# Rotary embedding on one core: rows in pairs, the last tile stored whole, 63 no-ops at the top of two programs

## The chip, the cores and the metric

The kernel runs on one core of a Trainium2 chip. The metric is the device time of one execution in microseconds (us); the time before is the median of 13 runs. The core has five engines that run their own instruction streams and meet at semaphores: PE (matrix multiply), DVE (VectorE), ACT (ScalarE), POOL (GpSimd) and SP, which here only issues DMAs. Sixteen DMA engines, called rings below, move data between the HBM and the on-chip memory SBUF. PSUM is a smaller on-chip memory that PE writes its results to[...].

## What is computed

```
def setup_inputs():
    batch, seq, dim = (16, 512, 1024)
    num_heads = 16
...
x = x.reshape(batch, seq, num_heads, head_dim)
x1, x2 = (x[..., :half_dim].copy(), x[..., half_dim:].copy())
...
rotated = np.concatenate([x1 * cos - x2 * sin, x1 * sin + x2 * cos], axis=-1)
```

Everything is fp32. `x` and the output are 33.6 MB each; `cos` and `sin` are 512 x 32 tables, one row for each position of the sequence. Each element of the output is one product with cos and one product with sin (of the element in the other half of its head), added.

## The kernel before

**Tiles.** Two batches make a tile of 128 partitions: 64 partitions for each batch, and on each partition 8 rows of 1024 elements that lie one behind the other in HBM (32 KB). There are 8 tiles, numbered t = 0 to 7, in a pool of 5 buffers (`BUFS`), and a tile is changed in place: loaded, rotated, stored from the same buffer. One DMA of a whole tile moves 4 MB, a piece of 32 KB for each partition.

**The SP queue.** All loads and stores are issued by SP, in program order: rows 0 to 2 of tile 0, the sin and cos tables, the rest of tile 0, tiles 1 to 4 (L75, L84, L85), and then the stores (L79). After the store of tile 2 come the loads of tiles 5, 6 and 7, each of which waits until the store that frees its buffer (tile 0, 1, 2) has landed. An instruction of SP that waits holds up all that is behind it. The last tile is stored in two halves, `LAST_OUT = (4, 8)`: rows 0 to 3 as soon as they are done, then rows 4 to 7.

**The tables.** One identity matrix doubled (L106) and two matmuls (L107, L108) spread the 64-partition tables over 128 partitions in the PSUM tile `tab`. DVE makes `sns` from it in SBUF (L110, L111), sin with a minus sign for the first half of a head, and one row of that back in `tab` (L115).

**The rows of a tile** go one by one, k = 0 to 7, in one of three ways:

- Rows 1, 2, 3, 5, 6 and 7: POOL multiplies the row, halves swapped, by sin into a buffer `b` (L168). DVE multiplies the row by cos into the PSUM tile `pd` (L186), and later adds the two into the row (`add`, L148). A list `pending` holds the addition back by a row or so.
- Row 4: the same product on POOL (L168); DVE makes the cos product in two halves of 512 into PSUM tiles `ps` (L174); PE adds `b` to each half by a matmul with the identity (L181), and ACT copies the half from PSUM into the row (L182).
- Row 0: as row 4, but DVE makes the sin product itself, in place (L179), and POOL does nothing.

So POOL has 7 products of 1024 elements for each tile, and DVE 17 instructions: 6 at L186, 6 at L148, 4 at L174, 1 at L179. There are 6 buffers `b`, 2 tiles `pd` (1024 elements) and 3 `ps` (512).

**Order between tiles.** `finish(t - 1)` is called after row 0 of tile t: it makes the addition that is still pending, and issues the store of tile t - 1. In the middle of the kernel (t = 3) ACT issues four small DMAs with 15, 14, 12 and 8 pieces of 64 bytes (L193); nothing reads what they load.

Of the kernel before, what the change touches and what calls it, by code (L numbers as in the profile page):

```python
# [8 lines left out]
FP32 = mybir.dt.float32  # L9
BF16 = mybir.dt.bfloat16  # L10
ALU = mybir.AluOpType

NB = 2
BUFS = 5
B_BUFS = 6
BANK = 512


PE_ROWS = ((0, 4), (0, 4))

DVE_B = ((0,), (0,))

FIRST = (3, 8)
LAST_OUT = (4, 8)

SMALL = (15, 14, 12, 8)


@with_exitstack
def kernel(  # L30
    ctx: ExitStack,
    tc: tile.TileContext,
    x: bass.AP,
    cos: bass.AP,
    sin: bass.AP,
    num_heads: bass.AP,
    out: bass.AP,
):

    nc = tc.nc
    P = nc.NUM_PARTITIONS
    batch, seq, dim = x.shape
    nh = num_heads
    hd = dim // nh
    half = hd // 2
    PB = P // NB  # L50
    KK = seq // PB
    NT = batch // NB
    F = KK * dim

    x_v = x.rearrange("(t b) (p k) d -> t (b p) (k d)", b=NB, k=KK)
    out_v = out.rearrange("(t b) (p k) h d -> t (b p) (k h d)", b=NB, k=KK)
    cos_v = cos.rearrange("(p k) j -> p (k j)", k=KK)
    sin_v = sin.rearrange("(p k) j -> p (k j)", k=KK)

    fixed = ctx.enter_context(tc.tile_pool(name="fixed", bufs=1))  # L60
    xp = ctx.enter_context(tc.tile_pool(name="xp", bufs=BUFS))
    bp = ctx.enter_context(tc.tile_pool(name="bp", bufs=B_BUFS))
    pfix = ctx.enter_context(tc.tile_pool(name="pfix", bufs=1, space=bass.MemoryType.PSUM))
    pe = ctx.enter_context(tc.tile_pool(name="pe", bufs=3, space=bass.MemoryType.PSUM))
    pd = ctx.enter_context(tc.tile_pool(name="pd", bufs=2, space=bass.MemoryType.PSUM))

    ctx.enter_context(tc.manual_schedule())

    tiles = [None] * NT

    def load(t, lo=0, hi=KK):
        if tiles[t] is None:
            tiles[t] = xp.tile([P, F], FP32, name="xt")
        s = slice(lo * dim, hi * dim)
        nc.sync.dma_start(out=tiles[t][:, s], in_=x_v[t][:, s])  # L75

    def store(t, lo=0, hi=KK):
        s = slice(lo * dim, hi * dim)
        nc.sync.dma_start(out=out_v[t][:, s], in_=tiles[t][:, s])  # L79

    load(0, 0, FIRST[0])
    sin_sb = bp.tile([P, dim], FP32, name="b")[:PB, : KK * half]
    cos_sb = bp.tile([P, dim], FP32, name="b")[:PB, : KK * half]
    nc.sync.dma_start(out=sin_sb, in_=sin_v)  # L84
    nc.sync.dma_start(out=cos_sb, in_=cos_v)  # L85
    for lo, hi in zip(FIRST, FIRST[1:]):
        load(0, lo, hi)
    for t in range(1, BUFS):
        load(t)

    ident = fixed.tile([P, P], FP32)
    make_identity(nc, ident)
    zero = fixed.tile([P, BANK], BF16)
    nc.vector.memset(zero, 0.0)  # L94
    for i in range(3):
        ps = pe.tile([P, BANK], FP32, name="ps")
        nc.tensor.matmul(out=ps, lhsT=zero[:, :P], rhs=zero, start=True, stop=True)  # L97

    spare = fixed.tile([16, len(SMALL), 16], FP32)
    sns = fixed.tile([P, KK, 2, half], FP32)  # L100
    tab = pfix.tile([P, BANK], FP32)
    cos_t = tab[:, : KK * half]
    sin_t = tab[:, KK * half : 2 * KK * half]
    spread = fixed.tile([PB, P], FP32)
    for b in range(NB):
        nc.vector.tensor_copy(out=spread[:, b * PB : (b + 1) * PB], in_=ident[:PB, :PB])  # L106
    nc.tensor.matmul(out=sin_t, lhsT=spread, rhs=sin_sb, start=True, stop=True)  # L107
    nc.tensor.matmul(out=cos_t, lhsT=spread, rhs=cos_sb, start=True, stop=True)  # L108
    sin_k = sin_t.rearrange("p (k j) -> p k j", k=KK)
    nc.vector.tensor_scalar_mul(out=sns[:, :, 0, :], in0=sin_k, scalar1=-1.0)  # L110
    nc.vector.tensor_copy(out=sns[:, :, 1, :], in_=sin_k)  # L111
    on_dve = sorted(set(DVE_B[0]) | set(DVE_B[1]))
    sns_t = tab[:, KK * half : KK * half + len(on_dve) * hd]
    for i, k in enumerate(on_dve):
        nc.vector.tensor_copy(out=sns_t[:, i * hd : (i + 1) * hd], in_=sns[:, k])  # L115

    def cos_b(k, n):
        c = cos_t[:, k * half : (k + 1) * half]
        return bass.AP(tensor=c.tensor, offset=c.offset, ap=[c.ap[0], [0, n], [1, half]])

    def over_heads(s):
        return bass.AP(tensor=s.tensor, offset=s.offset, ap=[s.ap[0], [0, nh], [1, hd]])

    def swapped(r, n):
        return bass.AP(
            tensor=r.tensor, offset=r.offset + half, ap=[r.ap[0], [hd, n], [-half, 2], [1, half]]
        )

    def swapped_signed(k):

        i = on_dve.index(k)
        s = sns_t[:, i * hd : (i + 1) * hd]
        return bass.AP(
            tensor=s.tensor, offset=s.offset + half, ap=[s.ap[0], [0, nh], [-half, 2], [1, half]]
        )

    def pairs(r):
        return r.rearrange("p (a j) -> p a j", j=half)

    def halves(r):  # L140
        return r.rearrange("p (h a j) -> p h a j", a=2, j=half)

    pending = []

    def add(most):
        while len(pending) > most:
            r, ps, b = pending.pop(0)
            nc.vector.tensor_tensor(out=r, in0=ps, in1=b, op=ALU.add)  # L148

    def finish(t):  # L150
        add(0)
        lo = 0
        for hi in LAST_OUT if t == NT - 1 else (KK,):
            store(t, lo, hi)
            lo = hi
        if t + 1 == NT - BUFS:
            for n in range(BUFS, NT):
                load(n)

    for t in range(NT):  # L160
        xt = tiles[t]
        for k in range(KK):
            r = xt[:, k * dim : (k + 1) * dim]
            own = k in DVE_B[t % 2]
            if not own:
                b = bp.tile([P, dim], FP32, name="b")
                sk = sns[:, k].rearrange("p a j -> p (a j)")
                nc.gpsimd.tensor_tensor(out=halves(b), in0=swapped(r, nh), in1=over_heads(sk), op=ALU.mult)  # L168
            if k in PE_ROWS[t % 2]:
                parts = []  # L170
                for c in range(0, dim, BANK):
                    ps = pe.tile([P, BANK], FP32, name="ps")
                    rc = r[:, c : c + BANK]
                    nc.vector.tensor_tensor(  # L174
                        out=pairs(ps), in0=pairs(rc), in1=cos_b(k, BANK // half), op=ALU.mult
                    )
                    parts.append((ps, rc, swapped(rc, BANK // hd) if own else b[:, c : c + BANK]))
                if own:
                    nc.vector.tensor_tensor(out=halves(r), in0=halves(r), in1=swapped_signed(k), op=ALU.mult)  # L179
                for ps, rc, rhs in parts:  # L180
                    nc.tensor.matmul(out=ps, lhsT=ident, rhs=rhs, start=False, stop=True, skip_group_check=True)  # L181
                    nc.scalar.copy(out=rc, in_=ps)  # L182
            else:
                add(1)
                ps = pd.tile([P, dim], FP32, name="pd")
                nc.vector.tensor_tensor(out=pairs(ps), in0=pairs(r), in1=cos_b(k, 2 * nh), op=ALU.mult)  # L186
                pending.append((r, ps, b))
            if k == 0 and t > 0:
                finish(t - 1)
            add(1)  # L190
        if t == NT // 2 - 1:
            for i, n in enumerate(SMALL):
                nc.scalar.dma_start(out=spare[:n, i], in_=sin_v[:n, :16])  # L193
    finish(NT - 1)


# [33 lines left out]
```

## Time and profile before

| | us |
|---|---|
| median of 13 runs | 162.5 (162.28 to 163.29) |
| the profiled execution | 162.66 |
| its span, first to last instruction | 160.9 |
| DVE busy | 141.4 (88% of the span) |
| POOL busy | 130.3 (81%) |
| PE busy | 62.1 (39%) |
| ACT busy | 20.0 (12%) |
| DMA packets, share of 16 rings | 97.8% of the span, 67.24 MB |

The span is shorter than the time of the same execution by 1.8 us, which lie before the first and behind the last instruction. An engine's busy time is the union of its instructions' times. The DMA share is the time of all packets over 16 rings times the span; a packet of a tile is one piece of one partition, 32 KB, or 16 KB where half a tile is stored.

### The profile page before, as it was taken

Reading aid. Unit: us, or ns where it says so; the run is one execution under the profiler, and the core shown is the slowest. Engines: PE = TensorE matmul, PEld = TensorE weight load, DVE = VectorE, ACT = ScalarE, POOL = GpSimd, SP = SyncE. Lnnn points to the kernel's source line nnn. Section 1 sums busy time; section 2 is a strip of 40 time slices with the busy share of each in tenths; the row PEclk is TensorE's granted clock in tenths of the full one; section 3 lists DMA queues with packets and bytes.
Section 4 is the critical chain, followed back from the end, with each engine's and each line's share of the span. In section 5 each row is a group of like instructions: output and inputs, shape, how many; then the busy total and the mean of one; then the engine's idle time right before and its main releaser. Section 6 shows DMA issues by size and latency. Waiting matters only on the chain. (4 is left out here: it accounts for less than half of the span.)

```text
span 160.9 us, 531 instructions
## 1 busy us (share of the span) xinstructions
PE 62.1 (39%) x71; PEld 19.9 (12%) x71; DVE 141.4 (88%) x142; ACT 20.0 (12%) x33; POOL 130.3 (81%) x62
## 2 busy tenths in 40 slices
PE   3136360536217350809044530817062712635000
PEld 0112010202011100202020200211020201120000
DVE  1059999999999999999999999999999999999700
ACT  0111120021102020111102020202011110202000
POOL 1039999999999999999999799999999799940000
PEclk9999955555856876595558555555555585557755
DMA  5999999999999899999999999999999999999993
GB/s 186 400 412 467 399 513 391 391 521 391 391 497 416 385 432 481 391 416 489 399 400 505 399 399 466 432 399 456 448 399 440 464 399 440 456 407 411 428 440 163
DMA packets 2852, 67.26 MB, mean 418 GB/s; under 512 B 418, under 2 KB 546, under 8 KB 546
## 3 DMA queue, kind: packets, MB, share of 16 engines
q1 hardware_dynamic: 2752, 67.24, 97.8%
q10 hardware_dynamic: 98, 0.00, 0.0%
q14 instruction: 2, 0.02, 0.0%
HBM read 33.69 MB, written 33.55 MB: 418 GB/s over the span
## 5 line engine op out<-in xcount | busy, mean ns | idle before, releaser
L168 POOL TENSOR_TENSOR b<-xt,sns 128x1024 f32<-128x1024 f32 x56 | 129.6, 2362 | 11.6 <-DVE sns L111 9.2
L186 DVE TENSOR_TENSOR pd<-xt,tab 128x1024 f32<-128x1024 f32 x48 | 58.1, 1225 | 0.8
L148 DVE TENSOR_TENSOR xt<-pd,b 128x1024 f32<-128x1024 f32 x48 | 58.4, 1217 | 0.0
L181 PE MATMUL ps<-xt,ident 128*128 128x512 f32 x32 | 29.6, 1079 | 49.1 <-issue 38.1
L181 PE MATMUL ps<-b,ident 128*128 128x512 f32 x32 | 29.0, 1061 | 29.7 <-DVE ps L174 27.1
L182 ACT COPY xt<-ps 128x512 f32<-128x512 f32 x32 | 18.8, 586 | 120.3 <-PE ps L181 120.3
L174 DVE TENSOR_TENSOR ps<-xt,tab 128x512 f32<-128x512 f32 x32 | 20.6, 688 | 0.0
L181 PEld LDWEIGHTS ps<-xt,ident 128*128 128x128 f32 x32 | 9.4, 324 | 68.7 <-issue 64.1
L181 PEld LDWEIGHTS ps<-b,ident 128*128 128x128 f32 x32 | 9.1, 312 | 49.4 <-issue 25.4
L179 DVE TENSOR_TENSOR xt<-xt,tab 128x1024 f32<-128x1024 f32 x8 | 9.8, 1222 | 0.4
L110 DVE TENSOR_SCALAR sns<-tab 128x256 f32<-128x256 f32 x1 | 0.4, 425 | 8.1 <-PE tab L108 8.1
L107 PE MATMUL tab<-b,spread 64*128 64x256 f32 x2 | 1.2, 696 | 5.0 <-DMA b<-in_sin_dram 5.0
L182 ACT ACT_TABLE_LOAD x1 | 1.3, 1283 | 7.4 <-DMA xt<-in_x_dram 7.4
L97 PE MATMUL ps<-zero 128*128 128x512 bf16 x3 | 1.5, 626 | 1.2 <-DVE zero L94 1.2
L107 PEld LDWEIGHTS tab<-b,spread 64*128 64x128 f32 x2 | 0.5, 306 | 5.8 <-issue 5.8
L108 PE MATMUL tab<-b,spread 64*128 64x256 f32 x2 | 1.1, 631 | 0.0
L94 DVE MEMSET zero<- 128x256 uint32 x1 | 0.3, 272 | 0.9 <-PEq L211 0.9
L108 PEld LDWEIGHTS tab<-b,spread 64*128 64x128 f32 x2 | 0.7, 333 | 0.2
L106 DVE COPY spread<-ident 64x64 f32<-64x64 f32 x2 | 0.3, 184 | 0.2 <-POOL ident masks.py:199 0.2
L97 PEld LDWEIGHTS <-zero 128*128 128x128 bf16 x3 | 0.3, 125 | 1.5 <-DVE zero L94 1.2
masks.py:197 POOL MEMSET ident<- 128x128 f32 x1 | 0.2, 204 | 0.3 <-POOLq L211 0.3
L111 DVE COPY sns<-tab 128x256 f32<-128x256 f32 x1 | 0.4, 415 | 0.0
(6 smaller groups left out, 0.9 us busy)
## 6 DMA issues: line engine op xcount, KB each, us to landing
xt<-in_x_dram SPq DMA_DIRECT2D x7, 4096.0 KB, 29.2
out_dram<-xt SPq DMA_DIRECT2D x7, 4096.0 KB, 28.0
out_dram<-xt SPq DMA_DIRECT2D x2, 2048.0 KB, 8.6
xt<-in_x_dram SPq DMA_DIRECT2D x1, 2560.0 KB
xt<-in_x_dram SPq DMA_DIRECT2D x1, 1536.0 KB, 6.6
b<-in_sin_dram SPq DMA_DIRECT2D x1, 64.0 KB, 6.3
b<-in_cos_dram SPq DMA_DIRECT2D x1, 64.0 KB, 5.9
spare<-in_sin_dram ACTq DMA_DIRECT2D x1, 0.9 KB, 7.2
```

The costliest lines, as they stand in the source:

```text
L97: nc.tensor.matmul(out=ps, lhsT=zero[:, :P], rhs=zero, start=True, stop=True)
L107: nc.tensor.matmul(out=sin_t, lhsT=spread, rhs=sin_sb, start=True, stop=True)
L108: nc.tensor.matmul(out=cos_t, lhsT=spread, rhs=cos_sb, start=True, stop=True)
L110: nc.vector.tensor_scalar_mul(out=sns[:, :, 0, :], in0=sin_k, scalar1=-1.0)
L111: nc.vector.tensor_copy(out=sns[:, :, 1, :], in_=sin_k)
L148: nc.vector.tensor_tensor(out=r, in0=ps, in1=b, op=ALU.add)
L168: nc.gpsimd.tensor_tensor(out=halves(b), in0=swapped(r, nh), in1=over_heads(sk), op=ALU.mult)
L174: nc.vector.tensor_tensor(out=pairs(ps), in0=pairs(rc), in1=cos_b(k, BANK // half), op=ALU.mult)
L179: nc.vector.tensor_tensor(out=halves(r), in0=halves(r), in1=swapped_signed(k), op=ALU.mult)
L181: nc.tensor.matmul(out=ps, lhsT=ident, rhs=rhs, start=False, stop=True, skip_group_check=True)
L182: nc.scalar.copy(out=rc, in_=ps)
L186: nc.vector.tensor_tensor(out=pairs(ps), in0=pairs(r), in1=cos_b(k, 2 * nh), op=ALU.mult)
```

## The change

- Rows 1 and 2, 4 and 5, 6 and 7 are handled two at a time: one POOL product, one DVE cos product and one DVE addition of 2048 elements for each pair. `pd` becomes one tile of 2048 elements.
- Row 3 takes the place of row 4 as the row that PE adds and ACT copies, in two halves that share one PSUM tile `pe_ps`.
- Row 0 has its cos product in one instruction of 1024 elements into `own_ps`, made in the tile before (for tile 0, ahead of the loop). PE adds it in two halves as before; ACT copies it in one instruction.
- The order inside a tile is written out. `pending` and `finish` are gone: the store of tile t is issued at the end of tile t.
- There are 3 buffers `b`, of 2048 elements. The tables' load takes one of them.
- The last tile is stored by one DMA.
- The four small DMAs of ACT are gone. Five DMAs with one piece of 64 bytes are issued by SP behind the load of tile 4; nothing reads what they load.
- The two copies at L106 become one.
- 63 no-op instructions stand at the top of DVE's program, and 63 at the top of POOL's.

```diff
-PE_ROWS = ((0, 4), (0, 4))
-DVE_B = ((0,), (0,))
+ROW_OWN, ROW_PE = 0, 3
+PAIRS = ((1, 2), (4, 5), (6, 7))
 FIRST = (3, 8)
-LAST_OUT = (4, 8)
-SMALL = (15, 14, 12, 8)
+LAST_OUT = (8,)
+EXTRA = 5
...
-    bp = ctx.enter_context(tc.tile_pool(name="bp", bufs=B_BUFS))
+    bp = ctx.enter_context(tc.tile_pool(name="bp", bufs=3))
...
-    pe = ctx.enter_context(tc.tile_pool(name="pe", bufs=3, space=bass.MemoryType.PSUM))
-    pd = ctx.enter_context(tc.tile_pool(name="pd", bufs=2, space=bass.MemoryType.PSUM))
+    pe = ctx.enter_context(tc.tile_pool(name="pe", bufs=1, space=bass.MemoryType.PSUM))
+    pd = ctx.enter_context(tc.tile_pool(name="pd", bufs=1, space=bass.MemoryType.PSUM))
...
     for t in range(1, BUFS):
         load(t)
+    spare = fixed.tile([1, EXTRA, 16], FP32)
+    for i in range(EXTRA):
+        nc.sync.dma_start(out=spare[:1, i], in_=sin_v[:1, :16])
+    for i in range(63):
+        nc.vector.nop(hint="pause")
+    for i in range(63):
+        nc.gpsimd.nop(hint="pause")
...
+    def sin_product(out, r, k, n):
+        s = sns[:, k : k + n].rearrange("p k a j -> p (k a j)")
+        if n == 1:
...
+        else:
+            sb = bass.AP(tensor=s.tensor, offset=s.offset, ap=[s.ap[0], [hd, n], [0, nh], [1, hd]])
+            o = out.rearrange("p (k h a j) -> p k h a j", k=n, a=2, j=half)
+            i = bass.AP(
+                tensor=r.tensor,
+                offset=r.offset + half,
+                ap=[r.ap[0], [dim, n], [hd, nh], [-half, 2], [1, half]],
+            )
+        nc.gpsimd.tensor_tensor(out=o, in0=i, in1=sb, op=ALU.mult)
+
+    def sin_rows(t, k, n):
+        b = bp.tile([P, 2 * dim], FP32, name="b")[:, : n * dim]
+        sin_product(b, rows(t, k, n), k, n)
+        return b
+
+    def pe_half(k, r, b):
+        cos_product(pe_ps, r, k)
+        pe_add(pe_ps, b)
+        nc.scalar.copy(out=r, in_=pe_ps)
+
+    def pair_product(t, k):
+        ps = pd.tile([P, 2 * dim], FP32, name="pd")
+        cos_product(ps, rows(t, k, 2), k, 2)
+        return ps, rows(t, k, 2)
+
+    def pair_sum(ps, r, b):
+        nc.vector.tensor_tensor(out=r, in0=ps, in1=b, op=ALU.add)
...
+    cos_product(own_ps, rows(0, ROW_OWN), ROW_OWN)
     for t in range(NT):
...
+        first, second, third = PAIRS
+        b1 = sin_rows(t, first[0], 2)
+        p1 = pair_product(t, first[0])
+        r0 = rows(t, ROW_OWN)
+        own_product(r0)
+        for ps, r in zip(parts(own_ps), parts(r0)):
+            pe_add(ps, swapped(r))
+        nc.scalar.copy(out=r0, in_=own_ps)
+        b3 = sin_rows(t, ROW_PE, 1)
+        b2 = sin_rows(t, second[0], 2)
+        pair_sum(*p1, b1)
+        h0, h1 = zip(parts(rows(t, ROW_PE)), parts(b3))
+        pe_half(ROW_PE, *h0)
+        p2 = pair_product(t, second[0])
+        b1 = sin_rows(t, third[0], 2)
+        pair_sum(*p2, b2)
+        pe_half(ROW_PE, *h1)
+        p1 = pair_product(t, third[0])
+        if t + 1 < NT:
+            cos_product(own_ps, rows(t + 1, ROW_OWN), ROW_OWN)
+        pair_sum(*p1, b1)
+        stores(t)
```

`cos_product`, `own_product` and `pair_sum` run on DVE, `sin_product` on POOL, `pe_add` is a matmul with the identity on PE. `stores(t)` issues the store of tile t and, behind that of tile 2, the loads of tiles 5 to 7, as `finish` did.

## The prediction, made before the result was known

> **What bounds the kernel now.** I read the page first: the rows of slices, the DMA queues, the costliest groups.
>
> ```profile
> DVE  1059999999999999999999999999999999999700
> ...
> POOL 1039999999999999999999799999999799940000
> ...
> DMA  5999999999999899999999999999999999999993
> ...
> q1 hardware_dynamic: 2752, 67.24, 97.8%
> ...
> q14 instruction: 2, 0.02, 0.0%
> ...
> L168 POOL TENSOR_TENSOR b<-xt,sns 128x1024 f32<-128x1024 f32 x56 | 129.6, 2362 | 11.6 <-DVE sns L111 9.2
> ```
>
> Three things are full at once: DVE, POOL (less so) and the rings. The DMA row has no hole between its first and last slice, so the rings, not DVE, set the time. What is left to win is only what lies before the first packet, behind the last one, and any difference between rings. The busy time of each engine in stretches shows the end:
>
> ```profile
> core 0: us, PE busy (x) PEld busy (x) DVE busy (x) ACT busy (x) POOL busy (x), PEclk, DMA share, GB/s
> 154.10:158.20 4.10, 0.00 (x0) 0.00 (x0) 0.00 (x0) 0.00 (x0) 0.00 (x0) 0.50 1.04 448
> 158.20:158.60 0.40, 0.00 (x0) 0.00 (x0) 0.00 (x0) 0.00 (x0) 0.00 (x0) 0.50 0.29 123
> 158.60:158.90 0.30, 0.00 (x0) 0.00 (x0) 0.00 (x0) 0.00 (x0) 0.00 (x0) 0.50 0.01 0
> 158.90:159.20 0.30, 0.00 (x0) 0.00 (x0) 0.00 (x0) 0.00 (x0) 0.00 (x0) 0.50 0.13 55
> 159.20:160.90 1.70, 0.00 (x0) 0.00 (x0) 0.00 (x0) 0.00 (x0) 0.00 (x0) 0.50 0.00 0
> ```
>
> A packet counts where it starts. 0.13 x 0.30 us x 16 rings is 0.62 us: one packet (the packet records give 0.611 us for 16 KB, 1.213 for 32 KB), alone, starting after 158.9 when no other ring has anything left. The records put its end at 159.70; one other ring ends at 159.15, all others between 158.4 and 158.8. So one late ring costs 0.9 us. Why is it late? The only foreign packets in the run are the two of the instruction queue, which the DMA view of 54.3 to 54.8 us and of 97.9 to 98.4 us shows one each:
>
> ```profile
> q14 instruction: 1, 0.01, 4.0%
> ```
> ```profile
> q14 instruction: 1, 0.01, 3.9%
> ```
>
> By the records these took 0.318 and 0.309 us, and the data packet behind the first took 1.695 us instead of 1.213: 0.8 us lost on one ring, 0.6 on another, which are the two that end late. Last, the timeline of the end and of one tile on DVE:
>
> ```profile
> 149.54 2.35 DVE L148 TENSOR_TENSOR xt<-pd,b 128x1024 f32<-128x1024 f32 x2
> 151.97 0.33 SPq L79 DMA_DIRECT2D out_dram<-xt  x1
> ```
> ```profile
> 99.05 1.22 DVE L179 TENSOR_TENSOR xt<-xt,tab 128x1024 f32<-128x1024 f32 x1
> ...
> 103.58 1.22 DVE L148 TENSOR_TENSOR xt<-pd,b 128x1024 f32<-128x1024 f32 x1
> 104.83 1.23 DVE L186 TENSOR_TENSOR pd<-xt,tab 128x1024 f32<-128x1024 f32 x1
> 105.97 1.22 DVE L148 TENSOR_TENSOR xt<-pd,b 128x1024 f32<-128x1024 f32 x1
> ...
> 116.71 1.22 DVE L179 TENSOR_TENSOR xt<-xt,tab 128x1024 f32<-128x1024 f32 x1
> ```
>
> DVE ends at 151.89; half a tile is issued at 151.97 and needs 2.1 MB / 430 GB/s = 4.9 us of the rings, which reach it about 153.7. DVE is thus just ahead of the rings: a second, nearly equal bound.
>
> **Part by part. Pairs on DVE.** A tile takes 116.71 - 99.05 = 17.66 us. Starts of 1024-element instructions lie 1.134 us apart (105.97 to 104.83: 1.14), and those of the 512-element halves at L174 0.598 in the trace: 512 elements more cost 0.536 us, about 0.96 a ns, so 1024 take 1.067 and 0.066 us is fixed. L148 to L186 is 1.25 instead, 0.118 more, because the second waits for the first. Check: 15,360 elements are 16.0 us, 17 x 0.066 = 1.12, three such waits 0.35 and one of 0.12 before L179: 17.6. After the change a tile has the same elements in 10 instructions, and two waits for the instruction directly ahead (addition to next pair's product, since there is one `pd`; second pair's product to its addition): 16.0 + 0.66 + 0.24 = 16.90, so 0.76 less. [...] The starts say that consecutive instructions overlap by about 0.09 us, so I take the starts. [...]
>
> **First tile.** The tables are ready at the same time; DVE starts at 10.74, POOL at 10.53. A pair on POOL: the row's successive starts are 2.31 apart (thirteen in 30.09 us), so at most 4.62 if the row scales[...]. I take 4.62. POOL makes pair 1, row 3, pair 2: pair 2 is ready at 10.53 + 4.62 + 2.31 + 4.7 = 22.2, and DVE, which is at 20.3, waits. What follows until the next tile is 8.45 us (2.20 + 0.60 + 2.20 + 1.13 + 2.32): tile 1 starts at 30.6.
>
> **Waits that the change adds.** With 3 buffers the next tile's first product on POOL waits for PE's second half of row 3, and row 3 and pair 2 are queued behind it; DVE's second addition waits for the latter. Loop: DVE half 0.69, PE and its semaphores 2.13 (L181 to L182: 2.08), POOL 2 x 4.62 + 2.31 + 0.15, addition 2.20: 16.7 us against DVE's 16.90. POOL has 0.2 us to spare a tile, so up to 4.71 for a pair nothing stands still. The second half of row 3 now waits on DVE for ACT's copy of the first (one `pe_ps`), and all of DVE is queued behind it: PE 2.08 + copy 0.59 = 2.7, under 4.4 us of other DVE work; without this cover it would cost 2.7 a tile. Row 0's PSUM tile is read by ACT 5 us before DVE writes it again.
>
> **End of DVE.** 30.6 + 6 x 16.90 = 132.0 for the start of tile 7; its last addition starts 13.56 later and takes 2.29: 147.85, 4.0 us earlier than now. SP issues at 147.93.
>
> **Last tile whole.** 4.2 MB are 9.75 us of the rings, so it must be there when tile 6's store runs out. Rings without a late fetch run out at 158.4 to 158.8, less 9.75: 148.65 to 149.05. From issue to first packet: the first load is issued at 0.73, the records have its first packets at 1.74 to 2.45, so 1.0 to 1.7 us. The store reaches the rings at 148.95 to 149.65 and ends between 158.8 (rings decide) and 159.4; middle 159.1. Today's halves have no such gap; the price of the whole store is that any later DVE end counts in full.
>
> **No-ops and the fetch.** At 54.4 us DVE had run 49 instructions besides waits, at 98 us POOL 44 (busy counts of these stretches), so the fetches look like a position in the program that 63 more instructions would put into the first microseconds. There is no row for a no-op: between 17 ns (SP's shortest semaphore instruction) and some 100 (pairs of waits on POOL), 1.1 to 6.3 us. I take the low side, as they do nothing. They are covered: DVE is idle to 9.69 us, and its and POOL's setup (1.2 us) is needed by PE at 7.6 with 0.7 at the start, so up to about 90 ns each are free and each further 10 ns costs 0.63 us. A fetch before 1.7 us costs nothing; one that meets the first loads costs its ring 0.3 us, which ends it at 159.1, within the middle above. [...] The engines' timelines agree, no stall there; the ring does not, 0.8 us. I go by the ring.
>
> **Small things, at nothing.** ACT's four small DMAs put 98 packets of some 10 ns on the rings; five single pieces on SP's queue behind load 4 are at most 0.1 us on one ring. SP needs about 2.5 us to issue them, before its first store at 30 us. Stores come earlier by 3 to 4 us, but sit in a full queue; loads 6 and 7 still wait for landings at 72.6 and 82.6, which the rings set, and DVE needs tile 5 at 95, landed at 92.
>
> **Sum.** Last packet 159.70 to 159.1: 0.6 us. The profiled 162.66 becomes 162.06; the median is 0.16 lower: 161.9.
>
> **Rivals.** (1) *The fetch does not move*, because it is PE's (54 instructions by 54.4 us, no no-ops) or because it still hits a busy ring: that ring, free 0.9 late at 149.97, ends at 159.7 as now: 162.5. For it: the counts fit PE as well; against: POOL fits the second fetch best. (2) *POOL becomes the bound*, slower: its pair has one more dimension in its access pattern than any row here. From 4.62 on each further 0.1 costs the first tile 0.2 us (two pairs), and above 4.71 it costs each of the seven loops behind it 0.2 as well, 1.6 in all. DVE may end up to 148.2 to 148.9 before the present 159.70 is passed, so about 4.74 decides. At 5.0 us the end comes 4.8 us later, 152.7 + 1.8 + 9.75 = 164.2 for the last packet: 167.0. At 4.8 it is 163.8. (3) *Rings alone decide*, DVE being faster than my sum: 158.8, 161.6.
>
> **Numbers.** The forecast's case and (3): 0.58, 161.4 to 162.2. (1): 0.19, 162.2 to 162.8. (2), with slow no-ops: 0.23, from 162.8 up. About 0.2% (0.3 us) is what a measurement of this kernel tells from no change. Low 161.3, which all rings ending at 158.5 would give; high 163.5, which takes in the milder half of (2).
>
> **What would show it.** Right: both fetches before 3 us; tile pitch on DVE 16.9; last store issued near 147.9; no lone packet at the end. Wrong: a POOL pair over 4.7 us, DVE waiting for POOL in every tile, or a gap of over 1 us in the rings before the last store.

## The result, and the profile after

The changed kernel takes 163.34 us (median of 11 runs, 162.67 to 164.12), the kernel before 162.45 us beside it (48 runs, 162.25 to 163.36): ratio 1.0046, 95% interval 1.0034 to 1.0058. It is slower by 0.9 us by the medians (0.75 by the ratio) where 0.6 us less was forecast. Its runs also spread wider: the middle half of them spans 0.4 us against 0.15. The profiled execution, 162.83 us with a span of 161.0, is one of the quicker ones; a second one (e4_after_again) took 163.44.

First the page of the changed kernel: the rows of slices, the queues, the costliest groups.

```profile
DVE  0049969999999999999999999999999999998000
...
POOL 1039999999999999988998899898998899840000
...
DMA  5999999999999999999999999999999999999993
...
q1 hardware_dynamic: 2618, 67.24, 97.9%
q14 instruction: 3, 0.02, 0.0%
...
L169 POOL TENSOR_TENSOR b<-xt,sns 128x2048 f32<-128x2048 f32 (+1 forms) x32 | 126.4, 3982 | 12.1 <-DVE sns L121 6.7
L193 DVE TENSOR_TENSOR xt<-pd,b 128x2048 f32<-128x2048 f32 x24 | 54.9, 2286 | 2.4 <-POOL b L169 1.6
L145 DVE TENSOR_TENSOR pd<-xt,tab 128x2048 f32<-128x2048 f32 x24 | 55.0, 2291 | 0.2
```

The rings are as full as before, with no hole; DVE's last 9 stands a slice earlier. Two of the three packets of the instruction queue are fetches of 8 KB, the third is one of 40 bytes at the start. DVE waits for POOL once in the whole run (1.6 us, in tile 0). Now that wait, one tile on DVE and the end, from the timeline:

```profile
22.20 2.29 DVE L193 TENSOR_TENSOR xt<-pd,b 128x2048 f32<-128x2048 f32 x1 [1.58 <-POOL b L169]
...
98.54 2.30 DVE L145 TENSOR_TENSOR pd<-xt,tab 128x2048 f32<-128x2048 f32 x1
...
115.52 2.30 DVE L145 TENSOR_TENSOR pd<-xt,tab 128x2048 f32<-128x2048 f32 x1
```
```profile
146.21 2.29 DVE L193 TENSOR_TENSOR xt<-pd,b 128x2048 f32<-128x2048 f32 x1
148.56 0.33 SPq L78 DMA_DIRECT2D out_dram<-xt  x1
```

A tile takes 16.98 us (17.66 before), and DVE ends at 148.50, 3.4 us earlier. So the pairs make DVE faster, as they were meant to. The time is lost elsewhere. The start of the timeline shows what the no-ops take:

```profile
3.60 0.20 POOL masks.py:197 MEMSET ident<- 128x128 f32 x1 [3.16 <-issue]
...
4.23 0.27 DVE L101 MEMSET zero<- 128x256 uint32 x1 [4.23 <-issue]
```

These two instructions started at 0.73 and 0.85 before. In the trace a no-op follows the last after 47 ns on DVE and 40 on POOL, and behind some 60 of them stands one pause of 0.4 us on each engine, from 3.6 us on DVE and from 3.1 on POOL. The two fetches are then served far later than those pauses; these are the rows of the instruction queue in the DMA views of 7.5 to 8.5 us and of 8.5 to 9.5 us:

```profile
q14 instruction: 1, 0.01, 2.1%
```
```profile
q14 instruction: 1, 0.01, 2.1%
```

The packet records put them at 7.72 and 8.63 us, in the middle of tile 0's loads, and the data packet behind the second took 1.424 us where its like, of 20 KB, take 0.764. The end, as busy time in stretches:

```profile
157.00:158.20 1.20, 0.00 (x0) 0.00 (x0) 0.00 (x0) 0.00 (x0) 0.00 (x0) 0.50 1.01 437
158.20:158.60 0.40, 0.00 (x0) 0.00 (x0) 0.00 (x0) 0.00 (x0) 0.00 (x0) 0.50 0.19 82
158.60:159.00 0.40, 0.00 (x0) 0.00 (x0) 0.00 (x0) 0.00 (x0) 0.00 (x0) 0.50 0.00 0
```

0.19 x 0.40 x 16 is 1.2 us, one packet of 32 KB, started alone when all other rings had started their last; it ends at 159.81 by the records, the others by 159.34. The lone late ring is still there. In this execution it ends 0.1 us later than before (159.70); the middle of the other rings ends 0.6 us later, at 159.2 instead of 158.65. In the second profile the late ring ends at 160.39, with the others at 159.2 or earlier.

### The profile page after: what moved, and what is told of

Its sections match the earlier page's. It is cut to its first block, busy times and chain, and to the rows that moved or that the text cites. A ratio compares the mean times of both kernels' runs of the same rounds, so it can differ in the third digit from the quotient of the medians.

```text
span 161.0 us, 569 instructions
## 1 busy us (share of the span) xinstructions
PE 55.9 (35%) x71; PEld 18.4 (11%) x71; DVE 136.1 (85%) x85; ACT 18.4 (11%) x25; POOL 127.1 (79%) x38
## 4 chain that ended last, share of the span: by engine, by line
DVE 68%; issue 12%; POOL 7%; DMA 4%; PE 1%; SPq 0%; DVEq 0%
DVE xt L193 33%; DVE pd L145 31%; POOL b L169 7%; DMA b<-in_sin_dram 4%; DVE pe_ps L145 3%; PE tab L117 1%; PE tab L118 1%; DVE sns L120 0%; DVE xt L154 0%; DVE own_ps L145 0%; SPq L74 0%; DVE sns L121 0%; DVEq L193 0%
## 5 line engine op out<-in xcount | busy, mean ns | idle before, releaser
L169 POOL TENSOR_TENSOR b<-xt,sns 128x2048 f32<-128x2048 f32 (+1 forms) x32 | 126.4, 3982 | 12.1 <-DVE sns L121 6.7
L193 DVE TENSOR_TENSOR xt<-pd,b 128x2048 f32<-128x2048 f32 x24 | 54.9, 2286 | 2.4 <-POOL b L169 1.6
L145 DVE TENSOR_TENSOR pd<-xt,tab 128x2048 f32<-128x2048 f32 x24 | 55.0, 2291 | 0.2
L180 PE MATMUL own_ps<-xt,ident 128*128 128x512 f32 x32 | 29.2, 1069 | 57.8 <-DVE xt L154 52.1
L180 PE MATMUL pe_ps<-b,ident 128*128 128x512 f32 x32 | 24.7, 865 | 25.8 <-DVE pe_ps L145 25.8
L180 PEld LDWEIGHTS own_ps<-xt,ident 128*128 128x128 f32 x32 | 9.4, 324 | 74.8 <-DVE xt L154 60.1
L213 ACT COPY xt<-own_ps 128x1024 f32<-128x1024 f32 x8 | 8.1, 1012 | 76.1 <-PE own_ps L180 76.1
L185 ACT COPY xt<-pe_ps 128x512 f32<-128x512 f32 x16 | 9.4, 587 | 36.4 <-PE pe_ps L180 36.4
L145 DVE TENSOR_TENSOR pe_ps<-xt,tab 128x512 f32<-128x512 f32 x16 | 11.0, 686 | 0.0
L145 DVE TENSOR_TENSOR own_ps<-xt,tab 128x1024 f32<-128x1024 f32 x8 | 9.8, 1223 | 0.0
```

The lines of the kernel that those rows point to most:

```text
L145: nc.vector.tensor_tensor(out=o, in0=i, in1=cb, op=ALU.mult)
L169: nc.gpsimd.tensor_tensor(out=o, in0=i, in1=sb, op=ALU.mult)
L180: nc.tensor.matmul(out=ps, lhsT=ident, rhs=other, start=False, stop=True, skip_group_check=True)
L185: nc.scalar.copy(out=r, in_=pe_ps)
L213: nc.scalar.copy(out=r0, in_=own_ps)
```

## The experiments

Times are medians, beside the kernel before on the same chip (162.30 to 162.43 us). The theories' names are those of the texts on record. A: the whole last store comes too late. B, later T1 and M1: the early fetches make a ring late. C: the five small DMAs. T2: only the number of fetches counts. T3: the no-ops delay the tables. M2: only a fetch near 8 us is dear.

**e1_halves**

```diff
-LAST_OUT = (8,)
+LAST_OUT = (4, 8)
```

> The changed kernel with its last tile stored in halves again (rows 0 to 3, then 4 to 7), all else as changed. Theory A (the whole last store comes too late): in the profiled run of the changed kernel the rings have run out of tile 6 at about 149.0 us and the store's first packets start at 149.4 to 149.7. Half a tile issued near 146.9 covers that, the rings decide again, and jitter in DVE's end no longer counts: 0.5 to 1.0 us faster than the changed kernel, 162.3 to 162.8 us, with a narrower spread of runs. Theory B (the two instruction fetches, moved by the no-ops to 7.7 and 8.6 us, make one ring 0.9 us late and so set the end): no change, 163.3 us.

163.42 us (ratio 1.0055, 1.0042 to 1.0069): no gain. The last half was issued at 148.24 and the rings had no gap, but the last packet ended at 160.21, alone. A falls as the cause.

**e2_no_nops**

```diff
-    for i in range(63):
-        nc.vector.nop(hint="pause")
-    for i in range(63):
-        nc.gpsimd.nop(hint="pause")
```

> The changed kernel without the 63 no-ops on VectorE and the 63 on GpSimd. Theory A: the tables are ready up to 0.3 us earlier (11.07 instead of 10.74 us for the first product), so the end of VectorE and the time come 0.0 to 0.4 us earlier: 162.9 to 163.3 us; the gap in the rings before the last store stays. Theory B: with POOL's program under 64 instructions only one fetch is left, and it comes mid-run: the lone late ring is gone or less late, 162.5 us or less.

162.40 us (0.9998, 0.9990 to 1.0006), 0.9 us less than with them: all of the loss, as B says. One fetch is left, at 79.8 us; the last packet ends at 159.35.

**e3_no_extra**: the lines with `EXTRA` deleted.

> The changed kernel without the five small DMAs of SP. In the profile these wait for landings of the loads whose semaphores they reuse, and hold SP until 24.6 us; the first store is issued at 34.2 instead of 30.7 us. Theory A: the rings hold loads until 50 us, so this costs nothing: 163.3 us, within 0.2. Theory C (the small DMAs and the later stores cost time): faster by 0.5 us or more.

163.09 us (1.0040, 1.0026 to 1.0055), 0.25 less, with intervals that overlap. Without no-ops the same deletion went the other way (e8 against e7, +0.22). Against C, there is no run in which leaving them out gains time clear of noise. In e8 it cost 0.22 us, with intervals that lie apart; why is open.

**e4_after_again**: the changed kernel, nothing edited.

> The changed kernel once more, for its spread and a second profile beside the experiments. Theory A: 163.3 us, runs from 162.7 to 164.1, each run's time following VectorE's last addition plus about 12.5 us. Theory B: a profile in which the late ring is late by another amount, with no link to VectorE's end.

163.34 us (1.0046, 1.0031 to 1.0061). In its profile DVE ended 0.5 us earlier than in the first, and the last packet 0.6 us later: two profiles only, but the opposite of what A says.

**e5_before_whole**

```diff
 (the kernel before)
-LAST_OUT = (4, 8)
+LAST_OUT = (8,)
```

> The kernel before with its last tile stored by one DMA, all else as before. VectorE ends at 151.9 us there, the rings run out of tile 6 at about 149.0, a store reaches them 0.9 to 1.1 us after its issue and takes 9.75. Theory A: the last packet ends near 162.8 instead of 159.7: 3.0 us slower than before, 165.5 us. Theory B: no change, 162.5 us.

165.78 us (1.0203, 1.0190 to 1.0216): 3.5 more, A's price for a whole store behind DVE's end at 151.96. The rings stood still for 3.9 us in all, and then all of them ended within 0.15 us of each other: a wait before the last store lets a late ring catch up. So A's mechanism is real, and the pairs' earlier end keeps it small: in the profiles of the changed kernel with its last tile whole the rings stand still for 0.05 to 0.3 us before that store.

**e6_before_nops**: the kernel before with the four lines that e2 deletes.

> The kernel before with the 63 no-ops on VectorE and the 63 on GpSimd at the same place as in the change, all else as before. Theory A: the no-ops are covered; at most 0.3 us on the start of the rows, and VectorE's end is 0.7 to 1.7 us ahead of what the rings need: within 0.3 of 162.45 us. Theory B: the fetches come near 8 us instead of 54 and 98 us, a ring is as late as in the changed kernel: 0.5 to 0.9 us slower, 163.0 to 163.3.

163.70 us (1.0088, 1.0069 to 1.0108): 1.4 more, with no pair and no whole store in it. Besides the two early fetches, at 7.5 and 8.3 us, DVE's longer program has a third at 121 us, on the ring that ends last (160.48); so the 1.4 us are not the price of the early ones alone.

**e7_halves_no_nops**, e1's and e2's edits together, and **e8_halves_plain**, e3's as well:

> The changed kernel with the last tile in halves and without no-ops. Theory A: the rings alone decide: as e1_halves, or up to 0.3 us less by one fetch less, 162.0 to 162.6 us. Theory B: as e2_no_nops, the halves add nothing.

> The changed kernel with the last tile in halves, without no-ops and without the five small DMAs: the pairs alone. Theory A: as e7_halves_no_nops within 0.2 us, 162.0 to 162.6; it could be the fastest of all by one fetch less than the kernel before. Theory C (the small DMAs cost time): faster than e7_halves_no_nops by 0.3 us or more.

162.41 us (1.0005, 0.9997 to 1.0012) and 162.63 us (1.0022, 1.0015 to 1.0029). e7 lies where A had it, and also where B had it (e2: 162.40); e8 is just above. One fetch less than before gained nothing.

**e9_nops_dve** and **e10_nops_pool**: the loop on one engine kept, the other deleted.

> The changed kernel with the 63 no-ops on VectorE alone. VectorE fetches at about its 62nd instruction, GpSimd at about its 67th, which it does not reach without no-ops, so one fetch is left, early. Theory T1 (a fetch that meets tile 0's loads makes its ring 0.8 us or more late at once, and the ring stays late to the end): 162.9 to 163.3 us, nearly as slow as with both, since the latest ring counts and not the sum. Theory T2 (the number of fetches counts, not their place): one fetch as in e2_no_nops, 162.4 us. Theory T3 (the no-ops delay the tables and with them VectorE): 162.9, half way.

> The changed kernel with the 63 no-ops on GpSimd alone: its fetch comes early, VectorE's near 80 us as in e2_no_nops; two fetches. T1: 162.9 to 163.4 us. T2: as the changed kernel, 163.3. T3: 162.9. Together with e9_nops_dve and e11_nops_20 it tells T1 from T2.

163.62 us (1.0065, 1.0042 to 1.0087) and 162.27 us (0.9996, 0.9988 to 1.0004). The loss belongs to DVE's no-ops alone. T2 and T3 fall: with one fetch it is slow, and the first row product started at 10.73 us in both. T1 has the sign on DVE, though e9 lies 0.3 us above its range, and was wrong on POOL. The ends of the two in stretches, first e9:

```profile
158.60:159.00 0.40, 0.00 (x0) 0.00 (x0) 0.00 (x0) 0.00 (x0) 0.00 (x0) 0.50 0.02 0
159.00:159.40 0.40, 0.00 (x0) 0.00 (x0) 0.00 (x0) 0.00 (x0) 0.00 (x0) 0.50 0.19 82
```

A whole packet still starts after 159.0, at 159.24, when every other ring has ended (158.97). Then e10:

```profile
158.60:159.00 0.40, 0.00 (x0) 0.00 (x0) 0.00 (x0) 0.00 (x0) 0.00 (x0) 0.50 0.02 0
159.00:159.40 0.40, 0.00 (x0) 0.00 (x0) 0.00 (x0) 0.00 (x0) 0.00 (x0) 0.50 0.00 0
```

No data packet starts after 158.6 (0.02 is 0.13 us of small packets; in "after" each ring's last data packet is followed by one of 4 bytes that takes about 9 ns).

**e11_nops_20**: `range(63)` to `range(20)` in both loops.

> The changed kernel with 20 no-ops on each engine in place of 63. Both engines still pass the places where they fetch, VectorE near 50 us and GpSimd near 105 us: two fetches, both in the middle of the run. T1: like the kernel before with its two fetches at 54 and 98 us, 162.3 to 162.7 us. T2: two fetches as in the changed kernel, 163.3 us. T3: a third of the delay, 162.7.

162.21 us (0.9993, 0.9985 to 1.0001), the lowest of all: two fetches, at 54.3 and 108.8 us, and no loss. T1 held (0.1 us under its range), T2 fell again.

**e12_loads_later**

```diff
+    for i in range(100):
+        nc.sync.nop(hint="pause")
     load(0, 0, FIRST[0])
```

> The changed kernel with 100 no-ops at the top of SP's program, so that the first load is issued about 4 us later, near 5 us, when the two early fetches have had idle rings. T1: the fetches land at about 4 to 5 us, no ring is late by 0.8 us when tile 0 is loaded, and the last packet ends about 157.1 us after the first one, as without no-ops (e2_no_nops: 159.35 less 1.75 = 157.6), against 158.1 to 158.6 in the two profiles of the changed kernel; the time is 162.4 plus the delay, about 166.5 us. T2 and T3: the late ring, or the late tables, remain: 167.3 us.

167.63 us (1.0313, 1.0297 to 1.0330). The delay was larger than planned: the first packet came at 7.03 instead of 1.75 us. Less these 5.28 us it is 162.35, the time without no-ops, and the fetches did land ahead of the data, at 4.1 to 4.7 us. This fits T1, but weakly: the rings also stood still for 0.6 us before the last store, which lets a late ring catch up, a third fetch had come with SP's longer program, and in the profiled run, the slowest of four, the last packet ended 157.9 us after the first one, between the 157.6 and the 158.1 to 158.6 of the text on record. One packet at 114.8 us took 1.78 us instead of 1.21, with no fetch near it.

**e13_nops_dve_40** and **e14_nops_dve_50**: 40 and 50 no-ops on DVE, none on POOL.

> The changed kernel with 40 no-ops on VectorE and none on GpSimd: one fetch, VectorE's, at about 25 to 30 us, while whole tiles are loaded and well before the rings turn from loads to stores near 50 us. Theory M1 (a fetch costs its ring about 0.8 us wherever it falls, and a ring that is late pays again each time the rings turn, near 51 and 110 us, so an earlier fetch is dearer): between e2_no_nops and e9_nops_dve, 162.6 to 163.2 us. Theory M2 (only a fetch among tile 0's first loads, near 8 us, is dear, because the packet behind it is stretched by 0.66 us there): 162.2 to 162.4 us.

> The changed kernel with 50 no-ops on VectorE and none on GpSimd: its fetch at about 13 to 17 us, at the start of the whole-tile loads. M1: 162.8 to 163.4 us, not under e13_nops_dve_40. M2: 162.2 to 162.5 us.

163.58 us (1.0077, 1.0056 to 1.0099) and 163.39 us (1.0058, 1.0043 to 1.0072), with the fetch at 31.1 and 19.0 us. M2 falls. M1 has the sign, but a size too small for e13, which was no cheaper than a fetch at 8 us, and e14 is not dearer than e13. e13's end:

```profile
159.40:159.80 0.40, 0.00 (x0) 0.00 (x0) 0.00 (x0) 0.00 (x0) 0.00 (x0) 0.50 0.00 0
159.80:160.20 0.40, 0.00 (x0) 0.00 (x0) 0.00 (x0) 0.00 (x0) 0.00 (x0) 0.50 0.19 82
```

One ring begins its last 32 KB packet near 159.9 and ends at 161.13, 2.1 us behind the next (159.02).

**e15_nops_20_halves**: e11's and e1's edits together.

> The changed kernel with 20 no-ops on each engine and the last tile in halves: the best of the parts so far, as e11_nops_20 still shows a gap of 0.2 us in the rings before its last store. If the rings' end follows the gap: 0.0 to 0.2 us under e11_nops_20, 162.0 to 162.3 us, and 0.0 to 0.2% under the kernel before. If the one late ring decides anyway: no change, 162.2 to 162.4.

162.41 us (1.0003, 0.9993 to 1.0014): closing the gap before the last store gained nothing. No version beat the kernel before by more than the measurement tells; e11 and e10 equal it.

**Where a late ring loses its time.** From the packet records: the fetch's own packet, by how much the data packet behind it is longer than its like, and the stretched packets that stand about 1 us behind the pack when the rings turn from loads to stores, near 51.5 and near 110 us (us; "past": the fetch came after).

| run | DVE's fetch at | fetch + packet behind | near 51.5 | near 110 | last packet ends |
|---|---|---|---|---|---|
| before | 54.4 | 0.32 + 0.48 | past | 0.20 | 159.70 |
| e11 | 54.3 | 0.31 + 0.46 | past | none | 159.23 |
| e2 | 79.8 | 0.31 + 0.47 | past | none | 159.35 |
| after | 8.6 | 0.33 + 0.66 | none | 0.20 | 159.81 |
| e9 | 8.2 | 0.33 + 0.66 | 0.54 | 0.78 | 160.45 |
| e14 | 19.0 | 0.33 + 0.66 | 0.19 | 0.44 | 159.92 |
| e13 | 31.1 | 0.33 + 0.66 | 0.74 | 1.18 | 161.13 |

The records don't name the rings, but the next packet of a full ring starts within 15 ns of the end of the one before, so a ring can be followed. In "after", e2 and e11 this leads without a fork from the last packet back to the stretched one behind DVE's fetch, in "after" through the one near 110 as well. In e13 and e14 it leads without a fork from the fetch through both stretched packets, and then, with forks behind 111 us, to the end; in e9 and "before" only the place in time ties the row together. POOL's early fetch in e10 costs 0.31 + 0.35, and 0.33 near 110, and its ring too is the one that ends last (no fork), at 159.25, when the others end near 158.9.

So shown is that DVE's fetch costs its ring 0.99 to 1.03 us in every early case and 0.66 to 0.80 in every late one, that its ring pays again at the turns in e13 and e14 (1.9 and 0.6 us), and that in "after" this ring sets the end. In the rows of the changed kernel the ring ends 0.4 to 0.8 us less behind the middle of the others than its losses add up to, while in "before", with the last tile in halves, it ends as far behind (1.0 us) as it lost; the pause of the rings before a whole last store (0.2 to 0.3 us in these profiles) gives back a part. Why a ring that is behind is stretched at the turns is open, as is why DVE's early fetch stretches the next packet more than POOL's. The stretches at the turns vary from run to run, which would also account for the wide spread of the changed kernel.

## Why the prediction was wrong

- **What bounds the kernel**: right. The rings are full in every profile up to the last store, and, e5 apart, a late ring sets the end; where it could be followed to its start it is one with an instruction fetch. The prediction found it and then priced it wrongly. (Of the other rings in the profile of before, two and not one end at 159.15.)
- **Pairs on DVE**: right. 16.98 us a tile against 16.90 forecast from the starts: 0.68 us a tile were saved where 0.76 were expected.
- **POOL pair**: 4.47 us from start to start where nothing held it up, 0.15 under the 4.62 that was taken from two single rows; its record is 4.52. The loop with three buffers never held DVE up after tile 0, so rival 2 did not come.

```profile
L169 POOL TENSOR_TENSOR b<-xt,sns 128x2048 f32<-128x2048 f32 x24 | 108.3, 4524 | 12.1 <-DVE sns L121 6.7 <-DVE xt L193 5.5
```

- **End of DVE**: 148.50 against 147.85. The rows started 0.33 later in that execution (11.07 for 10.74; the experiments with the same no-ops have 10.56 to 10.81), but POOL's shorter pairs made up for it: tile 1 starts at 30.65, as forecast. The rest is 0.07 to 0.08 a tile and 0.16 in the last one. Small.
- **Last tile whole**: right in kind. In the busy times in stretches of the changed kernel, the rings run low before the store and all start on it together:

```profile
146.00:149.30 3.30, 0.04 (x1) 0.00 (x0) 2.40 (x2) 0.59 (x1) 0.00 (x0) 0.50 0.76 328
149.30:149.80 0.50, 0.00 (x0) 0.00 (x0) 0.00 (x0) 0.00 (x0) 0.00 (x0) 0.50 2.30 983
```

  Packets count where they start, so 2.30 means that nearly every ring starts one here. The gap is 0.3 us of all rings by the records, 0.05 to 0.3 in later runs. The middle of the rings, late one apart, ends at 158.7 to 159.2 with the whole store and at 158.6 to 158.8 with halves; still nothing is won by halves (e1), as the late ring then has no such gap to catch up in.
- **No-ops and the fetch**: this is the step that failed: "A fetch before 1.7 us costs nothing; one that meets the first loads costs its ring 0.3 us, which ends it at 159.1, within the middle above." The attribution held: DVE pauses behind 63 recorded instructions, POOL behind 68, and 63 no-ops do move both fetches (e6: none is left at 54 or 98 us). But the no-ops took 3.0 us on DVE and 2.5 on POOL, not the 1.1 of the low side, and a fetch was not served at the pause (3.6 and 3.1 us): its packet came 4 to 5 us later, in busy rings. And the price was mis-sized: 0.33 + 0.66 us at once for DVE's, and up to 1.9 more at the turns (e13), against 0.3 taken. I had counted the packet's own time and left out the stretched packet behind it, though the profile of before showed exactly that (1.695 for 1.213), and I held a ring's lateness to be the same wherever it begins. Rival 1 named the right mechanism, a fetch that "still hits a busy ring", but gave it the price of no change. That the price lies on the ring and not on the engines was right: at the fetches of the kernel before, DVE's instructions start 1.13 and 0.60 us apart around 54.4 us and POOL's 2.30 and 2.31 around 98, as elsewhere, while a fetch cost its ring between 0.58 us (POOL's in that run) and 1.03.
- **Small things**: right within 0.25 us.

Put together: without no-ops the change would have been worth nothing (e2: 0.9998) rather than 0.6 us. The 3.4 us that DVE gains stay off the critical path, since the rings need 157 us for the same bytes, and the part that was hoped for from the fetches did not come: a fetch late in the run, one or two, still leaves its ring last (159.35 in e2, 159.23 in e11, where 159.1 was forecast). The base was high as well: 159.70 is from an execution 0.2 us over the median of the 48 runs, and the 0.16 taken off at the end assumed that the same excess would stay.

## What to carry to other kernels

In a kernel whose DMA rings are full from end to end, look at the last microsecond ring by ring: the rings here did not share work (in e9 one starts 32 KB when all others have ended), so what holds one of them up, even an instruction fetch of 8 KB (0.58 to 1.03 us here), shows at the end, less what a pause of all rings gives back (in e5 they stood still for 3.9 us and ended within 0.15). The length of an engine's program decided where such a fetch fell (with 0, 20, 40, 50 and 63 no-ops on VectorE at 79.8, 54.3, 31.1, 19.0 and 8.2 us); here VectorE's, where it fell before the rings first turn from loads to stores, made the kernel 1.1 to 1.3 us slower (e9, e13, e14), and one in the middle left its ring 0.3 us behind the others (e2, e11), which cost nothing against the kernel before, where one ring ends 1.0 us behind. VectorE, made to end 3.4 us earlier behind such a bound, gained slack and not time (e2: ratio 0.9998): spend such slack on something or leave the kernel alone.

## What the runs showed of the hardware that was not expected

- A fetch goes with a place in the program: behind 63 recorded instructions on DVE and 68 on POOL stands the pause when no-ops run there, and 128 later on DVE comes the next fetch (e6: 121 us, at its 191st). In the kernel before the places are a few records lower (by the fetch's packet 58 on DVE, 64 on POOL).
- The packet follows the pause by 4.2 to 5.1 us when the rings are busy with tile 0, and by 1.1 to 1.2 us when they are idle (e12: pauses at 3.05, 3.56 and 3.57 us, packets at 4.14, 4.63 and 4.73).
- A no-op takes 18 ns on DVE and 13 on POOL by its record, but 47 and 40 from one to the next.
- When all rings turn from loads to stores near 50.5 us, some packets take 0.1 to 0.5 us longer than usual, without a fetch in sight: twelve in the kernel before (from 49.3 to 50.8 us), 28 in e15, none in "after" and e2.
- A wait of all rings before the last store evens them out: in e5 they ended within 0.15 us of each other, against 1.3 us before.
